# Identity products ahead of the first tile, an opening in halves, and a new order of weight blocks in a transformer trunk kernel

## The chip, the core and the metric

The kernel runs on one NeuronCore of a Trainium2 chip. The core has a matrix engine (TensorE, PE in the profile; its weight loads are shown apart as PEld), a vector engine (VectorE, DVE), a scalar engine (ScalarE, ACT), a general engine (GpSimd, POOL) and a sync engine (SyncE, SP) which issues most of the transfers. The engines run their own instruction streams in order and wait for each other through semaphores. 16 DMA engines move data between HBM, where weights and inputs lie, and the on-chip memory of 128 partitions. Matmul results go to banks of a separate accumulator memory.

The metric is the time of one execution on the device in microseconds, the median of several runs.

## What is computed

Two layers of a transformer trunk over two groups of requests, 256 and 512 rows of 1024 values, with the same weights. The first layer mixes tokens by windowed grouped attention with a sink, the second by differential attention; each is followed by a SwiGLU of hidden width 2816.

```python
def window_gqa_sink(h, w_in, w_o, sinks):
    q, k, v = jnp.split(h @ w_in, [A_Q_DIM, A_Q_DIM + A_KV_DIM], axis=-1)
    ...
    q = apply_rope(q, cos, sin) * (HEAD_DIM ** -0.5)
    k = apply_rope(k, cos, sin)
    ...
    m = jnp.maximum(jnp.max(sc, axis=-1, keepdims=True), sink)
    e = jnp.exp(sc - m)
    p = e / (jnp.sum(e, axis=-1, keepdims=True) + jnp.exp(sink - m))
    ...
    return o @ w_o

def swiglu(h, w_gate_up, w_down):
    g, u = jnp.split(h @ w_gate_up, 2, axis=-1)
    return (jax.nn.silu(g) * u) @ w_down

def trunk(x, ...):
    for i in range(DEPTH):
        h = rms_norm(x, norm_mix_pre[i])
        m = window_gqa_sink(...) if i % N_MIXERS == 0 else diff_attention(...)
        x = x + rms_norm(m, norm_mix_post[i])
        h = rms_norm(x, norm_ffn_pre[i])
        x = x + rms_norm(swiglu(h, ffn_w_gate_up[i], ffn_w_down[i]), norm_ffn_post[i])
    return x
```

## The kernel before

**Tiles and products.** The 768 rows are six tiles of 128 rows (0 and 1 the prompt, 2 to 5 the sample), in two halves of three tiles. Every fp32 product is made of three: an operand is split into a rounded part and a remainder (hi and lo), and hi·hi, lo·hi and hi·lo are summed in one bank (L376 to L378 in `product_steps`). The split of a weight block is an ACT cast (`whi`, L273) and a DVE subtraction (`wlo`, L274), together `two_parts`.

**Weight blocks.** `prepare` goes through a list of units in the order of their use. `fetch` issues the loads of the raw blocks on SP (L247) as far as buffers are free: two buffers "w" (tile name `wraw`) and two "y" (`y_wraw`), which are the scratch buffers that hold `y_pre`, `y_e` and the like at other times. A split block lies in one of RING = 5 pairs `whi`, `wlo`. `take` hands blocks to the products; `free` calls `prepare` again when a block is no longer needed, so the place of that call in the program is the place in ACT's and DVE's streams at which the next block's split stands. Units 0 to 3 are the k-v weights of the first mixer (768 columns), 4 to 12 its q and k weights, from 13 its output weights. For units 4 to 13, `whi` is not cast by ACT but loaded a second time from HBM by a converting DMA that POOL issues (L321); DVE's subtraction (L322) follows.

**Opening.** `enter(t)` normalizes a tile: sum of squares (ACT, L427), root (L420), power on POOL (L421), scaling by the row's factor and the gain `gpre` (`scaled`, DVE, L431) into `y_pre`. `transposes` turns it on PE with an identity (L469, bank `tp_h`), and the result is split again into the transposed operand (L364, L365). In the mixer tile t + 1's `entered` stands between the products of k-v unit t (`straight`), and loads the tile three ahead.

**First mixer.** `mixer_a` runs through 24 fills, groups of matmuls for k-v, q and k columns. Between these it places 96 items: each scores one head of one tile (bank `sc`, then DVE L800 and an exponential on ACT in buffer `y_e`), every second one normalizes the pair of heads two earlier (L811, L812; head one scaled on DVE, L814, head two on ACT, L815), the item four earlier is transposed (PE L832, bank `tpe`; copied to `eT` by ACT, L838), and values are summed (L847, bank `poa`). The table `marks` in `a_items` sets where items stand, in fills: item 6 stands at 9.6 of the 24 fills, item 24 at 13.7, with the others between by interpolation. `drop` frees a weight block as soon as its last product has been issued.

**Feed-forward part.** `ffn` multiplies by a scheme with seven products of quarter blocks for gate and up weights, for 11 pairs of column blocks. For the first AHEAD = 6 blocks (`for c in range(AHEAD)`) the two gate products p1 and p2 have been made earlier, and p6, p5, p7, p3, p4 follow, into the banks `py` and `pw`. They need the up block and sums of quarters of the gate and up block: `b11` (L309), `b12` (L310), `b22` (L311), `b21` (L312), made in place by DVE, with `two_parts` on them. ACT copies the results (`st` L1191, `u` L1196). The loads of gate and up blocks come in turn, all up blocks into "y" buffers but that of block c = 1.

**Tail.** The second feed-forward part ends with the last tile: `last_tile` normalizes the result by `rstd_last` and adds it to x (L568). That x is loaded by `begin(5)`, which is called inside the last product.

A scheduler keeps the order of the program on each engine but may hoist instructions whose operands allow it; `tc.issue_after(i)` puts what is issued in it behind instruction i.

Of the kernel before, what the change touches and what calls it, by code (L numbers as in the profile page):

```python
# [9 lines left out]
F32 = mybir.dt.float32  # L10
# [7 lines left out]
P = 128  # L18
# [32 lines left out]
def a_items():  # L51
# [4 lines left out]
    marks = ((0, 6.6), (6, 9.6), (24, 13.7), (48, 18.6), (72, 23.1), (76, 24))  # L56
# [32 lines left out]
def trunk(  # L89
# [107 lines left out]
    def ffn_units(layer):  # L197
        for c in range(AHEAD):
            plain(wgu[layer, c, 0], 1024)
        for c in range(NCH):  # L200
# [6 lines left out]
            raw_src.append((wgu[layer, c, 1], 1024, "w" if c == 1 else "y"))  # L207
# [30 lines left out]
    state = {"dma": 0, "split": 0, "used": 0, "w": 0, "y": 0, "tt": 0, "rb": 0, "cap": None, "behind": None, "after": None, "hold": False}  # L238
# [37 lines left out]
    def prepare(upto):  # L276

        while state["split"] < min(upto, len(units), state["cap"] or len(units)):
# [23 lines left out]
            else:  # L302
# [4 lines left out]
                b22s[i] = both[:, :512], both[:, 512:]  # L307
                two_parts(*b22s[i], b22)
                nc.vector.tensor_tensor(out=b11, in0=b12, in1=b11, op=ALU.subtract)  # L309
# [4 lines left out]
            with ExitStack() as after:  # L314
# [5 lines left out]
                if 4 <= i < N_PLAIN_A:  # L320
                    nc.gpsimd.dma_start(out=hi[:, :n], in_=raw_src[r][0])  # L321
                    state["raw_lo"] = nc.vector.tensor_tensor(  # L322
                        out=lo[:, :n], in0=src[:, :n], in1=hi[:, :n].bitcast(F32), op=ALU.subtract)
                else:
                    two_parts(hi[:, :n], lo[:, :n], src[:, :n])
# [365 lines left out]
    def mixer_a(gains, first_steps, o):  # L691
        with ExitStack() as st:
# [20 lines left out]

            def drop():
                live[0] -= 1
                free(live[0])
# [89 lines left out]
            def normalize(g, t, j):  # L806
# [7 lines left out]
                nc.vector.tensor_scalar(out=e[0], in0=e[0], scalar1=den[:, 0:1], scalar2=None, op0=ALU.mult)  # L814
# [46 lines left out]
            def item(n):  # L861
                if n < n_items:
                    score(*items[n])
                if n % 2 == 0 and 2 <= n <= n_items:
                    normalize(*items[n - 2])
                if LAG <= n < n_items + LAG:
                    turn_e(*items[n - LAG])
# [274 lines left out]
    def ffn(layer, later, comb, cpool, cstack, ostack, gains):  # L1142
# [219 lines left out]
        with ExitStack() as st:  # L1362
# [144 lines left out]
            if not final:  # L1507
# [11 lines left out]
                return {0: [do(4, 2), do(5, 1)], 1: [do(3, 3)], 2: [do(4, 3), do(5, 2)], 3: [do(5, 3)]}  # L1519
            ss4 = small.tile([P, 4], F32, tag="ss4", name="ss4")  # L1520
            junk = new_y("last")
            ss = sq[5][0]
            for k in range(2):
                last_product(2, gs, wk, last=True, parts=(k,))
                if k == 0:
                    stage(4, 1)
                    begin(5)
# [63 lines left out]
    nc.scalar.activation(out=warm, in_=mhalf[:, 0:1], func=AF.Square)  # L1591
    head = ctx.enter_context(ExitStack())
# [11 lines left out]
    def enter(t):  # L1604
        x = xs_sb[t]
        y_in[t] = new_y(f"pre0_{t}")
        scaled(y_in[t], x, row_rstd(x, y_in[t], f"pre0_{t}"), g_in)
# [10 lines left out]
    enter(0)  # L1618
    with tc.issue_after(state["rstd"].ins), tc.issue_after(state["scaled"].ins):
        prepare(2)  # L1620
    for s in transposes(y_in.pop(0), 0, "h0_0"):
        s()
# [103 lines left out]
```

## Time and profile before

| | us |
|---|---|
| runs | 1634.6, 1634.96, 1637.33 (median 1634.96) |
| profiled execution | 1637.23 |
| its span | 1635.4 |
| DVE busy in it | 1203.1 |
| ACT busy in it | 941.7 |
| POOL busy in it | 166.0 |

The span runs from the first to the last instruction that the profiler recorded; the time of the execution is 1.8 us longer. A row of the timeline gives the start and the duration in us, the engine (a q behind it marks a transfer's issue), the line, the operation, result and operands, and in brackets how long the engine was idle before it and for whom it waited. A row of the waits gives the waiting engine's line, what it waited for, the total, the number of waits and the longest. A row of the windows gives the stretch and its length, busy time and instruction count of PE, PEld, DVE, ACT and POOL, the granted PE clock, the share of the DMA engines and the traffic. The matmuls of the trace overlap, so durations of neighbours do not add up.

By the windows the first mixer's dense part, 80 to 240 us, has ACT busy for 135.70 of 160 us.

### The profile page before, as it was taken

Reading aid. Unit: us, or ns where it says so; the run is one execution under the profiler, and the core shown is the slowest. Engines: PE = TensorE matmul, PEld = TensorE weight load, DVE = VectorE, ACT = ScalarE, POOL = GpSimd, SP = SyncE. Lnnn points to the kernel's source line nnn. Section 1 sums busy time; section 2 is a strip of 40 time slices with the busy share of each in tenths; the row PEclk is TensorE's granted clock in tenths of the full one; section 3 lists DMA queues with packets and bytes.
Section 4 is the critical chain, followed back from the end, with each engine's and each line's share of the span. In section 5 each row is a group of like instructions: output and inputs, shape, how many; then the busy total and the mean of one; then the engine's idle time right before and its main releaser. Section 6 shows DMA issues by size and latency. Waiting matters only on the chain. (4 is left out here: it accounts for less than half of the span.)

```text
span 1635.4 us, 24441 instructions
## 1 busy us (share of the span) xinstructions
PE 1606.9 (98%) x9055; PEld 1491.6 (91%) x9055; DVE 1203.1 (74%) x2076; ACT 941.7 (58%) x1999; POOL 166.0 (10%) x261
## 2 busy tenths in 40 slices
PE   7999999999999999999999999999999999999998
PEld 7888778999999998888999999888999999998887
DVE  6778857878667766888585886857877667656985
ACT  5588976644444444556475666766644444444553
POOL 1121101000000000001220250421000000000000
PEclk9999999999999999999999999999999999999999
DMA  6532204443433257675432332504444432347674
GB/s 214 174 99 69 91 19 168 156 169 113 145 111 118 101 169 261 223 257 183 141 109 71 95 85 80 153 1 175 161 138 144 138 115 96 126 147 259 221 246 159
DMA packets 73383, 233.07 MB, mean 143 GB/s; under 512 B 9072, under 2 KB 17456, under 8 KB 73008
## 3 DMA queue, kind: packets, MB, share of 16 engines
q1 hardware_dynamic: 55008, 178.82, 32.1%
q0 software_dynamic: 18112, 52.44, 10.6%
q8 instruction: 71, 1.16, 0.3%
q14 instruction: 48, 0.39, 0.1%
q10 hardware_dynamic: 144, 0.26, 0.0%
HBM read 171.71 MB, written 42.86 MB: 131 GB/s over the span
## 5 line engine op out<-in xcount | busy, mean ns | idle before, releaser
L274 DVE TENSOR_TENSOR wlo<-wraw,whi 128x1024 fp32r<-128x1024 f32 (+1 forms) x159 | 188.4, 1189 | 176.7 <-ACT whi L273 175.9
L273 ACT CAST whi<-wraw 128x1024 fp32r<-128x1024 f32 (+1 forms) x159 | 162.4, 1025 | 117.5 <-PE py L377 53.1
L376 PE MATMUL py<-hhi,whi 128*128 128x384 f32 x480 | 160.8, 335 | 4.3 <-ACT u L1196 4.3
L378 PE MATMUL py<-hhi,wlo 128*128 128x384 f32 x480 | 160.3, 334 | 0.0
L377 PE MATMUL py<-hlo,whi 128*128 128x384 f32 x480 | 160.3, 334 | 0.0
L364 ACT CAST hhi<-araw 128x768 fp32r<-128x768 f32 (+1 forms) x74 | 57.5, 783 | 88.2 <-DMA araw<-act 80.8
L376 PEld LDWEIGHTS py<-hhi,whi 128*128 128x128 f32 x480 | 90.1, 188 | 5.6 <-ACT u L1196 5.6
L376 PE MATMUL pv<-whi,hhi 128*128 128x512 f32 (+1 forms) x240 | 92.4, 385 | 0.3 <-DVE yf L1408 0.3
L378 PE MATMUL pv<-whi,hlo 128*128 128x512 f32 (+1 forms) x240 | 92.2, 384 | 0.4 <-DVE hlo L365 0.4
L377 PE MATMUL pv<-wlo,hhi 128*128 128x512 f32 (+1 forms) x240 | 92.2, 384 | 0.0
L365 DVE TENSOR_TENSOR hlo<-araw,hhi 128x768 fp32r<-128x768 f32 (+1 forms) x74 | 65.2, 889 | 33.9 <-ACT hhi L364 33.6
L377 PEld LDWEIGHTS py<-hlo,whi 128*128 128x128 f32 x480 | 90.1, 188 | 0.0
L378 PEld LDWEIGHTS py<-hhi,wlo 128*128 128x128 f32 x480 | 90.1, 188 | 0.0
L1228 POOL DMA_DIRECT2D act<-st x22 | 19.3, 878 | 629.7 <-DVE st L1227 599.5
L376 PE MATMUL po<-whi,hhi 128*128 128x512 f32 x192 | 78.7, 410 | 0.0
L1023 ACT ACTIVATE be<-bsc,bmx 128x512 f32<-128x512 f32 (+1 forms) x96 | 58.8, 616 | 30.8 <-DVE bmx L1021 30.2
L376 PE MATMUL px<-hhi,whi 128*128 128x384 f32 x224 | 75.5, 337 | 0.2
L377 PE MATMUL po<-wlo,hhi 128*128 128x512 f32 x192 | 75.4, 392 | 0.0
L378 PE MATMUL po<-whi,hlo 128*128 128x512 f32 x192 | 75.2, 392 | 0.0
L378 PE MATMUL px<-hhi,wlo 128*128 128x384 f32 x224 | 74.9, 335 | 0.0
L377 PE MATMUL px<-hlo,whi 128*128 128x384 f32 x224 | 74.9, 334 | 0.0
L1021 DVE TENSOR_REDUCE bmx<-bsc 128x1 f32<-128x512 f32 (+1 forms) x96 | 55.3, 595 | 11.0 <-PE bsc L1017 10.7
(318 smaller groups left out, 4923.1 us busy)
## 6 DMA issues: line engine op xcount, KB each, us to landing
wraw<-in_wgu SPq DMA_DIRECT2D x58, 512.0 KB, 4.4
act<-st POOLq DMA_DIRECT2D x22, 1344.0 KB, 6.6
araw<-act SPq DMA_DIRECT2D x70, 384.0 KB, 3.9
y_wraw<-in_wgu SPq DMA_DIRECT2D x42, 512.0 KB, 3.8
wraw<-in_wd SPq DMA_DIRECT2D x40, 512.0 KB, 3.9
xd<-x SPq DMA_DIRECT2D x18, 512.0 KB, 2.8
x<-xd SPq DMA_DIRECT2D x18, 512.0 KB, 4.3
wraw<-in_wo SPq DMA_DIRECT2D x16, 512.0 KB, 3.5
```

What stands on the lines that cost most here:

```text
L273: state["raw_hi"] = nc.scalar.copy(out=hi, in_=src)
L274: state["raw_lo"] = nc.vector.tensor_tensor(out=lo, in0=src, in1=hi.bitcast(F32), op=ALU.subtract)
L364: state["hi"] = nc.scalar.copy(out=hi, in_=src)
L365: state["lo"] = nc.vector.tensor_tensor(out=lo, in0=src, in1=hi.bitcast(F32), op=ALU.subtract)
L376: nc.tensor.matmul(out, ah, bh, start=start and i == 0, stop=False, skip_group_check=more)
L377: nc.tensor.matmul(out, ah, bl, start=False, stop=False, skip_group_check=more)
L378: state["mm"] = nc.tensor.matmul(out, al, bh, start=False, stop=stop and i == last, skip_group_check=more)
L1021: nc.vector.tensor_reduce(out=mx, in_=s, axis=AX.X, op=ALU.max, negate=True)
L1023: nc.scalar.activation(out=e[:, :n * P], in_=s, func=AF.Exp, bias=mx, accum_out=den[:, c:c + 1])
L1228: nc.gpsimd.dma_start(out=at_hand[c // 4][:, :, c // 2 % 2], in_=out.pop(c // 2))
```

## The change

1. Twelve fp32 products of the identity with itself go to PE ahead of the first tile, into a bank of their own that nothing reads.
2. The opening works in halves: tile 0 is scaled in two halves of 512 columns, block 0 of the k-v weights is split in two halves of 384 columns, and the first half of the tile's transposes stands between these (`state["between"]`). Blocks 1 and 2 are prepared apart.
3. In the first mixer, units 5 to 8 are split as all others are, with the ACT cast in place of the converting DMA on POOL. Unit 4 and units 9 to 13 keep the DMA.
4. In the first mixer, once items run, `drop` only notes that a block is free (`owed`); the replacement is made after the next `normalize`. The DVE subtraction of the converted blocks is issued behind the scaling of `y_e` (`state["scale"]`).
5. In `marks`, item 6 moves from 9.6 to 9.9 fills.
6. In both feed-forward parts all up blocks go to "y" buffers, and from the first block on L309, the sum `b11`, stands ahead of the block's `two_parts`, issued behind the previous block's `wlo` (`state["raw_lo"]`).
7. The last tile's x is loaded before the last products into a raw weight buffer, in place of `begin(5)`.

```diff
-    marks = ((0, 6.6), (6, 9.6), (24, 13.7), (48, 18.6), (72, 23.1), (76, 24))
+    marks = ((0, 6.6), (6, 9.9), (24, 13.7), (48, 18.6), (72, 23.1), (76, 24))
...
-            raw_src.append((wgu[layer, c, 1], 1024, "w" if c == 1 else "y"))
+            raw_src.append((wgu[layer, c, 1], 1024, "y"))
...
+                with tc.issue_after(state["raw_lo"].ins) if state["after"] is not None else ExitStack():
+                    nc.vector.tensor_tensor(out=b11, in0=b12, in1=b11, op=ALU.subtract)
                 two_parts(*b22s[i], b22)
-                nc.vector.tensor_tensor(out=b11, in0=b12, in1=b11, op=ALU.subtract)
...
-                if 4 <= i < N_PLAIN_A:
+                if i == 4 or 9 <= i < N_PLAIN_A:
                     nc.gpsimd.dma_start(out=hi[:, :n], in_=raw_src[r][0])
+                    if state["scale"] is not None:
+                        after.enter_context(tc.issue_after(state["scale"].ins))
                     state["raw_lo"] = nc.vector.tensor_tensor(
                         out=lo[:, :n], in0=src[:, :n], in1=hi[:, :n].bitcast(F32), op=ALU.subtract)
                 else:
-                    two_parts(hi[:, :n], lo[:, :n], src[:, :n])
+                    for j in range(0, n, HALF if i == 0 else n):
+                        c = slice(j, j + HALF if i == 0 else n)
+                        two_parts(hi[:, c], lo[:, c], src[:, c])
+                        if i == 0 and j == 0:
+                            state["between"]()
...
+            owed = []
+
             def drop():
                 live[0] -= 1
-                free(live[0])
+                if state["scale"] is None:
+                    free(live[0])
+                else:
+                    owed.append(True)
...
-                nc.vector.tensor_scalar(out=e[0], in0=e[0], scalar1=den[:, 0:1], scalar2=None, op0=ALU.mult)
+                state["scale"] = nc.vector.tensor_scalar(out=e[0], in0=e[0], scalar1=den[:, 0:1], scalar2=None, op0=ALU.mult)
...
                     normalize(*items[n - 2])
+                    if owed:
+                        owed.clear()
+                        free(live[0])
...
+            x_of[5] = wpool.tile([P, 1024], F32, tag="wraw", name=f"x{sub}_5", bufs=RAW["w"])
+            load(x_of[5], x_at[sub][5])
...
                     stage(4, 1)
-                    begin(5)
...
+    busy = bank("busy")
+    for i in range(12):
+        nc.tensor.matmul(busy[:, :P], ident, ident, start=i == 0, stop=i == 11)
...
-        scaled(y_in[t], x, row_rstd(x, y_in[t], f"pre0_{t}"), g_in)
+        r = row_rstd(x, y_in[t], f"pre0_{t}")
+        for cols in [slice(0, 512), slice(512, D)] if t == 0 else [slice(0, D)]:
+            scaled(y_in[t][:, cols], x[:, cols], r, g_in[:, cols])
...
     enter(0)
+    state["between"], second = transposes(y_in.pop(0), 0, "h0_0")
     with tc.issue_after(state["rstd"].ins), tc.issue_after(state["scaled"].ins):
+        prepare(1)
+    with tc.issue_after(state["hi"].ins), tc.issue_after(state["lo"].ins):
         prepare(2)
-    for s in transposes(y_in.pop(0), 0, "h0_0"):
-        s()
+    second()
```

The change also moves instructions that its lines don't name. Three places follow; in the rows stand the line, the operation, the result and the operands, and a name's last number only tells tiles of one name apart. The changed file's lines have other numbers.

SP's stream in the opening, before: `x_3` is the load of tile 3, the `wraw` loads are the first two q blocks (units 4 and 5), `ropea` is a table of rotary factors.

```order
L247 DMA wraw_172<-in_waf 128x1024
L458 DMA x_3_159<-in_xs 128x1024
L247 DMA wraw_178<-in_waf 128x1024
L698 DMA ropea_238<-in_rope_b 128x768
L458 DMA x_4_267<-in_xs 128x1024
L458 DMA x_5_326<-in_xs 128x1024
```

The same place in the changed kernel:

```order
L247 DMA wraw_195<-in_waf 128x1024
L247 DMA wraw_201<-in_waf 128x1024
L705 DMA ropea_254<-in_rope_b 128x768
L465 DMA x_3_172<-in_xs 128x1024
L465 DMA x_4_283<-in_xs 128x1024
L465 DMA x_5_342<-in_xs 128x1024
```

Tile 3's load has moved from the second to the fourth place, behind the second weight block and the table.

DVE's stream in the first mixer, before, around the first scaling that ends a long wait of PE (`y_e_0_2`, L814); `wlo_863` is the subtraction of a weight block.

```order
L676 TENSOR_TENSOR qa_1_822<-zqa_1_791,qa_1_822 64x384 x2
L322 TENSOR_TENSOR wlo_863<-wraw_651,whi_862 128x1024
L663 TENSOR_TENSOR zqa_1_872<-xqa_1_868,ropea_238 128x384
L811 TENSOR_TENSOR den_0_2_832<-den_0_2_832 128x2
L800 ISA y_e_2_2_919,negm_2_2_920<-sc_2_2_916,mask,nsink 128x256
L800 ISA negm_2_2_920 128x1
L812 RECIPROCAL den_0_2_832<-den_0_2_832 128x2
L809 TENSOR_TENSOR den_1_2_880<-negm_1_2_879,sink 128x2
L666 TENSOR_TENSOR xqa_1_868<-xqa_1_868,ropea_433 128x384
L814 TENSOR_SCALAR y_e_0_2_830<-y_e_0_2_830,den_0_2_832 128x256
```

In the changed kernel the scaling is L826 and the subtraction L325:

```order
L683 TENSOR_TENSOR qa_1_832<-zqa_1_801,qa_1_832 64x384 x2
L812 ISA y_e_1_2_897,negm_1_2_898<-sc_1_2_894,mask,nsink 128x256
L812 ISA negm_1_2_898 128x1
L670 TENSOR_TENSOR zqa_1_871<-xqa_1_867,ropea_254 128x384
L823 TENSOR_TENSOR den_0_2_851<-den_0_2_851 128x2
L812 ISA y_e_1_2_897,negm_1_2_898<-sc_1_3_921,mask,nsink 128x256
L812 ISA negm_1_2_898 128x1
L824 RECIPROCAL den_0_2_851<-den_0_2_851 128x2
L673 TENSOR_TENSOR xqa_1_867<-xqa_1_867,ropea_449 128x384
L826 TENSOR_SCALAR y_e_0_2_849<-y_e_0_2_849,den_0_2_851 128x256
L325 TENSOR_TENSOR wlo_909<-wraw_667,whi_908 128x1024
```

The subtraction now stands right behind the scaling, and the items around it are one score earlier.

DVE's stream in the first feed-forward part, blocks c = 1 and 2, before. L309 to L312 are the sums, L274 the subtractions of the split, the lines above L1190 the work on the products.

```order
L309 TENSOR_TENSOR wraw_3561<-wraw_3622,wraw_3561 128x512
L274 TENSOR_TENSOR b_3681<-wraw_3622,b_3681 128x512
L310 TENSOR_TENSOR wraw_3622<-wraw_3622 128x512
L311 TENSOR_TENSOR wraw_3622<-wraw_3622,wraw_3561 128x512
L312 TENSOR_TENSOR wraw_3561<-wraw_3561,wraw_3622 128x512
L274 TENSOR_TENSOR wlo_3680<-wraw_3622,whi_3679 128x1024
L274 TENSOR_TENSOR wlo_3706<-wraw_3561,whi_3705 128x1024
L1198 TENSOR_TENSOR st_0_3703<-st_0_3703,u_0_3732 128x384
L1218 TENSOR_TENSOR u_0_3677<-pw_0_3690,u_0_3677 128x384
L274 TENSOR_TENSOR b_3780<-y_wraw_3711,b_3780 128x512
L1219 TENSOR_TENSOR st_0_3703<-u_0_3677,ga_0_3453 128x384
L309 TENSOR_TENSOR wraw_3709<-y_wraw_3711,wraw_3709 128x512
```

The same in the changed kernel:

```order
L309 TENSOR_TENSOR wraw_3577<-y_wraw_3579,wraw_3577 128x512
L372 TENSOR_TENSOR s4lo_3075<-oa_247,s4hi_3074 128x4x128
L274 TENSOR_TENSOR b_3701<-y_wraw_3579,b_3701 128x512
L311 TENSOR_TENSOR y_wraw_3579<-y_wraw_3579 128x512
L312 TENSOR_TENSOR y_wraw_3579<-y_wraw_3579,wraw_3577 128x512
L313 TENSOR_TENSOR wraw_3577<-wraw_3577,y_wraw_3579 128x512
L274 TENSOR_TENSOR wlo_3700<-y_wraw_3579,whi_3699 128x1024
L274 TENSOR_TENSOR wlo_3726<-wraw_3577,whi_3725 128x1024
L1213 TENSOR_TENSOR st_0_3723<-st_0_3723,u_0_3748 128x384
L309 TENSOR_TENSOR wraw_3640<-y_wraw_3642,wraw_3640 128x512
L1233 TENSOR_TENSOR u_0_3697<-pw_0_3710,u_0_3697 128x384
L274 TENSOR_TENSOR b_3796<-y_wraw_3642,b_3796 128x512
```

The up block of the sum for c = 1 is now in a `y_wraw` buffer, and the sum stands one row earlier, ahead of the last subtraction of the operand `s4lo`; the next block's L309 has moved up to right behind the first use of the products.

More of the change, by code (lines that the diff above doesn't have):

```diff
@@ L237, in trunk @@
     raws, parts, b22s = {}, {}, {}
-    state = {"dma": 0, "split": 0, "used": 0, "w": 0, "y": 0, "tt": 0, "rb": 0, "cap": None, "behind": None, "after": None, "hold": False}
+    state = {"dma": 0, "split": 0, "used": 0, "w": 0, "y": 0, "tt": 0, "rb": 0, "cap": None, "scale": None, "between": None, "behind": None, "after": None, "hold": False}
     tpool, dpool = [None], [None]
```

## The prediction

> **What bounds the kernel now.** I read the busy times first, then the waits of TensorE (PE), then the timeline around each wait.
>
> ```profile
> span 1635.4 us, 24441 instructions
> PE 1606.9 (98%) x9055; PEld 1491.6 (91%) x9055; DVE 1203.1 (74%) x2076; ACT 941.7 (58%) x1999; POOL 166.0 (10%) x261
> ```
>
> PE is busy for 1606.9 of 1635.4 us, so 28.5 us is all that the order of other work can win unless PE's own work changes. PE's waits say where that time lies (total, times, longest):
>
> ```profile
> PE tp_h L469 <- DVE y_pre L431: 8.0, 1, 8.0
> PE py L376 <- ACT u L1196: 4.3, 4, 1.6
> PE tpe L832 <- DVE y_e L814: 2.2, 2, 2.0
> PE tpe L832 <- ACT y_e L815: 1.2, 3, 0.6
> PE poa L847 <- ACT eT L838: 0.9, 2, 0.5
> PE sc L791 <- DVE qa L676: 0.6, 1, 0.6
> PE pw L376 <- ACT st L1191: 0.5, 1, 0.5
> ```
>
> The first is the start of the program, the tpe, poa and sc rows are the first mixer, the py and pw rows the first six blocks of the two feed-forward parts. Every part of the change aims at one of these rows, or at the tail.
>
> A wait costs PE more than its row says. Matmuls overlap:
>
> ```profile
> 12.78 0.52 PE L376 MATMUL pkva<-whi,hhi 128*128 128x384 f32 x1
> 13.10 0.52 PE L377 MATMUL pkva<-wlo,hhi 128*128 128x384 f32 x1
> ...
> 17.67 0.33 PE L376 MATMUL pkva<-whi,hhi 128*128 128x384 f32 x1
> 17.84 0.33 PE L377 MATMUL pkva<-wlo,hhi 128*128 128x384 f32 x1
> ```
>
> At full clock one starts every 0.17 us though each lasts 0.33, so a wait costs its listed idle plus 0.16. At 13 us the pitch is 0.32: PE runs at half rate there, although the clock column already reads 1.00.
>
> **Opening.** The first transposes wait for the whole normalized tile 0; the twelve identity products only fill PE's empty time ahead of them.
>
> ```profile
> 7.96 0.69 PE L469 MATMUL tp_h<-ident,y_pre 128*128 128x128 f32 x2 [7.96 <-DVE y_pre L431]
> ...
> 25.13 0.38 PE L469 MATMUL tp_h<-ident,y_pre 128*128 128x128 f32 x2
> ```
> ```profile
> 14.01 0.33 SPq L458 DMA_DIRECT2D x<-in_xs  x1
> ...
> 19.99 1.06 ACT L427 ACTIVATE y_pre<-x 128x1024 f32<-128x1024 f32 x1
> ...
> 22.47 1.28 DVE L431 SCALAR_TENSOR_TENSOR y_pre<-x,rstd_pre,gpre 128x1024 f32<-128x1024 f32 x1 [0.99 <-POOL rstd_pre L421]
> ```
> ```profile
> 18.00:21.00 3.00, 2.88 (x21) 2.57 (x20) 3.00 (x9) 2.07 (x5) 0.00 (x0) 1.00 1.03 390
> 21.00:22.00 1.00, 1.00 (x7) 1.00 (x6) 0.47 (x2) 1.00 (x6) 0.11 (x1) 1.00 0.75 290
> 22.00:23.00 1.00, 1.00 (x7) 1.00 (x7) 0.53 (x1) 0.20 (x1) 0.43 (x1) 1.00 0.19 78
> ```
>
> (In the window rows the last two columns are the DMA share and GB/s.) The halves of the first scaling bring PE's first work forward by about half of a 1.28 us pass, 0.6 us, and a shorter half-rate stretch may bring the first products forward further. But all of it ends at tile 3, whose transposes run at 25.13. Its load, issued at 14.01 ahead of a 512 KB weight block and a 384 KB rope table, now stands behind both on SP's queue. The DMA engines are full until 21 us, so 0.9 MB at 390 GB/s puts it 2.3 us later; traffic ends soon after 22. Before, the tile's square started at 19.99 and the scaling ended at 23.75, 3.76 later, of which 0.99 was a wait for POOL. The square waited for no load before, so the tile was there somewhat earlier than 19.99; I take 21.8 for it now. With 3.76 behind it, less a little of POOL's 0.99, the transposes follow at about 25.4: PE is ahead until then, waits, and goes on 0.3 later. I take **a loss of 0.3**. From the other side: if the load is not late, the 0.99 wait and the 0.58 cast that stood inside the chain are the most that can go, a gain of 1.5. At worst the tile lands at 22.3, 0.9 lost, and the wait drops the clock (1.6, next part): a loss of 2.5.
>
> [...]
>
> **First mixer to 80 us.** Three waits end here; the last drops the clock.
>
> ```profile
> 49.28 0.41 PE L376 MATMUL pqa<-hhi,whi 128*128 128x384 f32 x1 [0.15 <-DMA whi<-in_waf]
> ...
> 63.50 0.50 PE L791 MATMUL sc<-ka,qa 128*128 128x256 f32 x2 [0.62 <-DVE qa L676]
> ...
> 73.82 0.87 PE L832 MATMUL tpe<-ident,y_e 128*128 128x128 f32 x3 [1.99 <-DVE y_e L814]
> ```
> ```profile
> 70.64 1.23 DVE L322 TENSOR_TENSOR wlo<-wraw,whi 128x1024 fp32r<-128x1024 f32 x1
> ...
> 73.33 0.35 DVE L814 TENSOR_SCALAR y_e<-y_e,den 128x256 f32<-128x256 f32 x1
> ```
> ```profile
> 74.00:77.00 3.00, 3.00 (x12) 3.00 (x12) 2.08 (x9) 2.95 (x8) 1.08 (x2) 0.50 0.35 133
> 44.00:80.00 36.00, 33.24 (x201) 31.46 (x201) 27.45 (x87) 22.16 (x69) 7.54 (x14) 0.95 0.60 197
> 80.00:240.00 160.00, 157.43 (x995) 131.96 (x994) 121.23 (x422) 135.70 (x396) 18.31 (x33) 1.00 0.22 68
> ```
>
> With the pitch the waits cost 0.3, 0.8 and 2.15. After the last the granted clock is 0.50 for 3 us, which holds 1.5 us of work, about 1.6 with its edges: 4.8 in all. At 73.82 PE waits for the scaling of y_e, and 1.23 us of block subtraction stands ahead of that scaling on DVE. The change puts the subtraction behind it, and spreads the items before it over 3.3 fills instead of 3.0, which moves this transpose later. The scaling then ends about 1.2 us earlier and the 1.99 falls to about 0.7, which I take as too short for the clock to fall; the other two waits leave 0.4 of 1.1, since whi of four blocks comes from an ACT cast of a buffer already here. Four casts of 1.02 us (the group row below) make ACT's 22.16 us here 26.3 of 36, and that is the cover. Gain 4.8 − 0.7 − 0.4 = **3.7**. If the denser queue takes all but 0.5 back it is 0.5; at best 4.8.
>
> [...]
>
> ```profile
> L273 ACT CAST whi<-wraw 128x1024 fp32r<-128x1024 f32 (+1 forms) x159 | 162.4, 1025 | 117.5 <-PE py L377 53.1
> ```
>
> **80 to 240 us.** Six waits remain (the 1.2 and 0.9 rows above and 0.2 of the y_e row); with 0.16 each, 3.2 us. Subtractions behind the scalings, in the order of the new code, help the DVE one and whatever queues on DVE. But ACT scales every second head, is busy 135.70 of 160, and gets nothing off its hands. Here the new order shows no row that prices it: I take **0.8**, a quarter, with 3.2 at best; at worst the deferred blocks come late at five of the fills by 0.46 each, minus 2.3.
>
> **Feed-forward.** The second up block used to be loaded into a buffer of the gate blocks, one place later:
>
> ```profile
> 309.42 0.33 SPq L247 DMA_DIRECT2D y_wraw<-in_wgu  x1
> 310.75 0.33 SPq L247 DMA_DIRECT2D wraw<-in_wgu  x1
> ```
> ```profile
> 315.26 0.69 DVE L309 TENSOR_TENSOR wraw<-wraw,wraw 128x512 f32<-128x512 f32 x1 [1.67 <-DMA wraw<-in_wgu]
> ...
> 1174.91 0.69 DVE L309 TENSOR_TENSOR wraw<-wraw,wraw 128x512 f32<-128x512 f32 x1 [2.31 <-DMA wraw<-in_wgu]
> ...
> 1210.71 0.69 DVE L309 TENSOR_TENSOR wraw<-y_wraw,wraw 128x512 f32<-128x512 f32 x1 [5.33 <-DMA wraw<-in_wgu]
> ```
> ```profile
> 320.46 0.45 PE L376 MATMUL py<-hhi,whi 128*128 128x384 f32 x1 [1.02 <-ACT u L1196]
> ...
> 1180.10 0.44 PE L376 MATMUL py<-hhi,whi 128*128 128x384 f32 x1 [1.64 <-ACT u L1196]
> ...
> 1214.39 0.44 PE L376 MATMUL py<-hhi,whi 128*128 128x384 f32 x1 [1.46 <-ACT u L1196]
> ```
>
> Now that block takes the earlier slot, 1.33 us sooner, and DVE's 1.67 wait shrinks to 0.3. The chain behind it (sums, subtraction of wlo) fed PE's wait at 320.46. The first part's py waits are 4.3 − 1.64 − 1.46 = 1.2, with two pitches 1.5; I leave 0.3 for the new order of ACT's copies: **1.2** (0 if ACT ends last anyway, 1.5 at best).
>
> In the second part two mechanisms work. At 1174.91 it is the same load. At 1210.71 the first sum of the next block (L309) had been hoisted ahead of the last sum and the wlo of this block, waited 5.33 us for a load not needed yet, and held them. The change issues each L309 behind the previous wlo, so that such a wait stands behind what PE needs next. The waits are 1.64, 1.46 and the pw row's 0.5: with pitches 4.1. I take **3.9**, leaving 0.2. If only the pw wait goes, 0.5; at best 4.1.
>
> **Tail.** The last tile's x used to be loaded late:
>
> ```profile
> 1629.81 0.55 POOL L421 TENSOR_TENSOR rstd_last<-rstd_last,mhalf 128x1 f32<-128x1 f32 x1 [3.39 <-ACT rstd_last L420]
> ...
> 1630.94 1.41 DVE L568 SCALAR_TENSOR_TENSOR x<-yf,rstd_last,x 128x512 f32<-128x512 f32 x2 [1.14 <-DMA x<-xd]
> ```
>
> With x there, the last pass follows POOL's end at 1630.36: 0.55 at most, nothing at least; I take **0.5**.
>
> **Sum.** −0.3 + 3.7 + 0.8 + 1.2 + 3.9 + 0.5 = 9.8. The profiled execution took 1637.23 us, which gives 1627.4. It is 2.27 above the median of the runs shown, 1634.96; from that the sum gives 1625.2, or 1626.8 if those runs lacked the 1.6 of the clock's fall. I forecast **1626.0**.
>
> **Rivals.**
> - *The opening gains.* The half-rate stretch shortens and tile 3 is not late, because transfers in flight share the DMA engines. 1.2 of the 1.5 bound instead of −0.3 gives 1624.5. For it: 5.1 us or more at half pitch hold 2.6 us of work. Against it: tile 3 is now last in a full queue. [...]
> - *The mixer's waits come back elsewhere.* The denser items use up what the scaling won, the clock falls at another place, and the 3.7 + 0.8 are nothing: 1630.5. For it: DVE is busy 27.45 of 36 us, ACT 26.3 with the casts.
> - *It doesn't do what it says.* The earlier buffer frees no sooner than the old one, and the feed-forward's 5.1 stay: 1631.1. Against it: the issue at 309.42 went into just such a buffer.
> - *Slower.* The deferred block replacement and the casts put work in front of ACT's and DVE's softmax steps at each of the 48 pairs of items. PE has no slack at 98%. At 0.3 us a pair, 14.4 us turn the gain into 1640.4; the median of before is passed from 0.19 a pair, 1638.2 from 0.25. Against it: in 80 to 240 us DVE idles 38.8 us and ACT 24.3, and PE waited six times.
>
> **Chances.** Forecast 0.62, opening 0.14, mixer 0.13, not as said 0.06, slower 0.05. The range must take in the second and third rival and a bound at a time: 80 to 240 at its worst costs 3.1 more (1629.1), the second part 3.4 more (1629.4), the first mixer 3.2 more (1629.2), and the two bases are 1.6 apart. To the other side the best of 80 to 240 gives 1623.6, with the opening's best 1621.8. So **1621.0 to 1631.5**. A measurement of this kernel tells about 0.2% from no change, 3.3 us: faster is below 1631.7, which the forecast, both gaining rivals and the mixer's meet, and most of the fourth: 0.88. Within 0.2%: 0.07. Slower, above 1638.2: 0.05.
>
> **What would show it.** Right: tile 3's transposes near 25.4 with a PE wait ahead of them; no granted clock of 0.50 near 75; no py wait over 0.4; an L568 row released by POOL. Wrong: new tpe or sc waits of a microsecond between 44 and 240, an L309 wait that still ends a PE wait, or transposes of tile 3 at 26 or later with the half pitch behind them.

## The result, and the profile after

| | runs | median, us | range, us |
|---|---|---|---|
| before | 6 | 1635.39 | 1634.6 to 1637.33 |
| changed | 6 | 1629.2 | 1625.55 to 1629.48 |

The ratio of the times is 0.9949, 95% interval 0.9938 to 0.9960: faster by 0.5%, 6.2 us between the medians. The profiled executions are 8.1 us apart (1637.23 and 1629.1). The forecast was 1626.0 with a range of 1621.0 to 1631.5; the median lies in it, 3.2 above the forecast.

The head of the page of the changed kernel (busy time, share and instructions of each engine):

```profile
span 1627.1 us, 24494 instructions
PE 1606.3 (99%) x9079; PEld 1492.8 (92%) x9079; DVE 1204.4 (74%) x2078; ACT 944.2 (58%) x2004; POOL 168.3 (10%) x257
```

PE is busy for the same time as before, though it has the identity products to do as well (24 rows of the trace, 5.5 us, in time that was empty). What fell is idle time. PE's waits in the changed kernel, over the whole span (total, times, longest):

```profile
PE tp_h L476 <- DVE y_pre L438: 3.8, 4, 2.0
PE busy L1610 <- POOL ident masks.py:199: 1.7, 1, 1.7
PE tpe L844 <- DVE y_e L826: 1.5, 2, 1.3
PE tp_h L476 <- DVE y_pd L438: 1.4, 1, 1.4
PE tpe L844 <- DVE den L821: 0.9, 1, 0.9
PE pv L383 <- DVE yf L1423: 0.8, 2, 0.5
PE pw L383 <- ACT st L1206: 0.7, 2, 0.4
```

The py row (4.3 us in four waits) is gone, and sc is too. tp_h now has four waits in the opening, one of 2.0 us at tile 3. The tpe row on den is new: a wait of 0.87 us at 78.48, in the first mixer. The two rows on y_pd and yf, which belong to places that the change doesn't touch, have grown.

To read where the time went, I take the **lead**: the start of a PE instruction in the profile of before minus the start of the same instruction in another profile. It is positive where the other kernel is ahead. The places are tile 3's transposes (before: 25.13), the first product of the second q block (49.28), two scores (100.02 and 201.06), a product of the first feed-forward part (352.63), the first product past 800, and the wait of the second part (1214.39). At these places every kernel's stream on PE has the same instructions behind it. Between 49 and 96 us that isn't so, since the table `marks` and the deferral shift the items against the products: the score at 81.15 comes six instructions later in the changed kernel. The figures 1.1 and 2.85 in the expectations below are leads read at 81 us; the lead is read at 100 here, and no wait of PE lies between 82 and 100 us in either kernel.

| kernel | tile 3 | 49 | 100 | 201 | 353 | 800 | 1214 | time (runs) |
|---|---|---|---|---|---|---|---|---|
| changed | −1.0 | −0.5 | 1.8 | 4.0 | 5.1 | 4.3 | 8.4 | 1629.2 (6) |
| f0_changed_again | −2.2 | −3.2 | −1.4 | 0.7 | 1.6 | 1.3 | 4.9 | 1629.03 (7) |
| e1_no_identity | 1.7 | 1.7 | 2.9 | 3.4 | 4.4 | 6.5 | 9.7 | 1627.26 (4) |
| e2_tile3_first | −0.5 | 0.0 | 2.4 | 4.5 | 5.9 | 8.0 | 11.8 | 1626.21 (5) |
| f1_tile3_first_again | −0.8 | −1.8 | 0.2 | 2.6 | 3.8 | 5.9 | 10.1 | 1626.82 (5) |
| e2b_tile3_first_no_identity | 1.4 | 0.6 | 2.9 | 3.2 | 4.3 | 5.5 | 9.5 | 1628.13 (4) |
| f2_no_identity_marks96 | 1.7 | 0.9 | 2.4 | 4.6 | 5.7 | 5.6 | 9.6 | 1627.22 (5) |
| e3_dma_whi | −0.6 | −1.9 | −0.8 | 1.4 | 2.5 | 2.5 | 6.6 | 1630.08 (1) |
| e4_marks96 | −0.4 | 0.0 | 1.9 | 3.8 | 4.9 | 6.9 | 11.1 | 1626.0 (1) |
| e5_free_at_drop | −0.9 | −0.4 | 1.8 | 1.2 | 2.2 | 4.0 | 8.0 | 1628.74 (1) |
| e6_up1_w | −0.9 | −2.0 | −0.8 | 1.0 | 0.0 | 0.1 | 2.1 | 1634.62 (1) |
| e7_sum_behind | −0.9 | −0.5 | 1.7 | 3.9 | 4.1 | 4.2 | 7.4 | 1629.32 (1) |
| f3_x5_late | −0.7 | −0.3 | 1.9 | 4.0 | 5.1 | 4.8 | 8.6 | 1629.34 (1) |

Each row is one profiled execution, so stages that a kernel shares with others tell how much a stage scatters. From 353 to 800 all of them run the same instructions, and the step of the lead there lies between −0.8 (changed) and +2.1 (e1, e2). No part of the change is read off that stage.

### The profile page after: what moved, and what is told of

Same layout as the page of the kernel before. It is cut to its first block, busy times and chain, and to the rows that moved or that the text cites. A ratio compares the mean times of both kernels' runs of the same rounds, so it can differ in the third digit from the quotient of the medians.

```text
span 1627.1 us, 24494 instructions
## 1 busy us (share of the span) xinstructions
PE 1606.3 (99%) x9079; PEld 1492.8 (92%) x9079; DVE 1204.4 (74%) x2078; ACT 944.2 (58%) x2004; POOL 168.3 (10%) x257
## 5 line engine op out<-in xcount | busy, mean ns | idle before, releaser
L274 DVE TENSOR_TENSOR wlo<-wraw,whi 128x1024 fp32r<-128x1024 f32 (+2 forms) x162 | 191.1, 1183 | 186.0 <-ACT whi L273 185.0
L273 ACT CAST whi<-wraw 128x1024 fp32r<-128x1024 f32 (+2 forms) x162 | 164.8, 1020 | 109.6 <-PE py L384 53.1
L274 DVE TENSOR_TENSOR wlo<-y_wraw,whi 128x1024 fp32r<-128x1024 f32 x44 | 53.8, 1223 | 13.8 <-ACT whi L273 13.7
```

Of the source, the lines that this page charges most:

```text
L273: state["raw_hi"] = nc.scalar.copy(out=hi, in_=src)
L274: state["raw_lo"] = nc.vector.tensor_tensor(out=lo, in0=src, in1=hi.bitcast(F32), op=ALU.subtract)
```

## Experiments

Times of the kernel before beside them: median 1636.35 (9 runs) with e1 to e3, 1635.56 (1 run) with e4 to e7, 1636.95 (12 runs) with f0 to f3. A kernel of one run is read by its profile only.

### e1_no_identity: without the identity products

```diff
-    busy = bank("busy")
-    for i in range(12):
-        nc.tensor.matmul(busy[:, :P], ident, ident, start=i == 0, stop=i == 11)
```

> The changed kernel without its twelve identity products, nothing else. Theory A (the products open the clock, but the opening ends at tile 3's load): the first k-v products run at a pitch of 0.32 us again until about 13 to 16 us, yet tile 3's transposes start within 0.3 us of the changed kernel's 26.16, because that tile lands at 22.2 in both, and PE's wait ahead of them shrinks from 2.0 to under 1; the time stays within 0.5 us of the changed kernel's. Theory B (the early clock is worth its time): the transposes start 1 to 2 us later, and the time grows by as much.

Both theories failed, at their common ground that tile 3 lands at the same time. Rows of the opening's timeline without the products (the issues on SP, the square of tile 3 on ACT, its transposes on PE):

```profile
13.64 0.33 SPq L465 DMA_DIRECT2D x<-in_xs  x1
14.02 0.42 SPq L247 DMA_DIRECT2D wraw<-in_waf  x1
14.50 0.44 SPq L705 DMA_DIRECT2D ropea<-in_rope_b  x1
...
18.65 1.06 ACT L434 ACTIVATE y_pre<-x 128x1024 f32<-128x1024 f32 x1 [0.20 <-DMA x<-in_xs]
...
23.48 0.38 PE L476 MATMUL tp_h<-ident,y_pre 128*128 128x128 f32 x2
```

The same rows of the changed kernel:

```profile
10.89 1.30 SPq L247 DMA_DIRECT2D wraw<-in_waf  x2
13.22 0.33 SPq L705 DMA_DIRECT2D ropea<-in_rope_b  x1
13.64 12.73 SPq L465 DMA_DIRECT2D x<-in_xs  x3
...
22.25 1.06 ACT L434 ACTIVATE y_pre<-x 128x1024 f32<-128x1024 f32 x1 [3.28 <-DMA x<-in_xs]
...
26.16 0.52 PE L476 MATMUL tp_h<-ident,y_pre 128*128 128x128 f32 x3 [1.99 <-DVE y_pre L438]
```

In both, tile 3's load is issued at 13.64, about when its buffer comes free (in the changed kernel tile 1's scaling on DVE, which reads that buffer, runs from 12.15 to 13.43). With the identity products the two others stand ahead of it and the tile is there at 22.25, without them at 18.65. So it is the identity products, not the halves, that put the load last. Why the order of SP's queue changes with them, no run shows. The transposes start 2.7 us earlier without the products.

And the products' own worth is small. Without them the half pitch (0.32 us from product to product) lasts until 11.33, 4.0 us from the first transposes at 7.31, in place of none:

```profile
10.70 0.53 PE L384 MATMUL pkva<-wlo,hhi 128*128 128x384 f32 x1
11.02 0.53 PE L385 MATMUL pkva<-whi,hlo 128*128 128x384 f32 x1
11.33 0.44 PE L383 MATMUL pkva<-whi,hhi 128*128 128x384 f32 x1
11.61 0.34 PE L384 MATMUL pkva<-wlo,hhi 128*128 128x384 f32 x1
11.79 0.34 PE L385 MATMUL pkva<-whi,hlo 128*128 128x384 f32 x1
```

Yet the lead near 16 us is 1.6 here and 1.8 in the changed kernel, because the full pitch there (0.17 us) runs into waits for the splits of the first operands (0.26, 0.16 and 0.45 us). The time, 1627.26, is 0.9944 of the kernel before (0.9930 to 0.9957); the changed kernel has 0.9949 in its own runs, so the medians don't tell them apart.

### e2_tile3_first: the load's place alone

```diff
-            load(raw[:, :n], src)
+            with tc.issue_after(state["x"].ins) if i == 5 else ExitStack():
+                load(raw[:, :n], src)
...
-        nc.sync.dma_start(out=x, in_=x_at[sub][t])
+        state["x"] = nc.sync.dma_start(out=x, in_=x_at[sub][t])
...
-                nc.sync.dma_start(out=full[:, :2 * HALF], in_=rope_b[len(tab)])
+                with tc.issue_after(state["x"].ins) if not tab else ExitStack():
+                    nc.sync.dma_start(out=full[:, :2 * HALF], in_=rope_b[len(tab)])
```

> The changed kernel with tile 3's load ahead of the second q block and of the table on SP's queue, as before. Theory A (the load's place costs the opening): the tile lands at about 19, PE has no wait at its transposes, which start at about 24.0 in place of 26.16; the time falls by 1.5 to 2.2 us against the changed kernel. Rival: the chain of square, root, power and scaling is as late as the load, or the second q block is late instead; the transposes start at 25 or later, or a new wait of PE stands between 28 and 45, and the time falls by less than 0.7.

The tile was there by 19.6, but the transposes started at 25.67 and not at 24.0. The wait moved one product up. DVE and PE of this kernel:

```profile
22.18 1.28 DVE L439 SCALAR_TENSOR_TENSOR y_pre<-x,rstd_pre,gpre 128x1024 f32<-128x1024 f32 x1 [0.66 <-POOL rstd_pre L429]
...
23.58 0.68 DVE L373 TENSOR_TENSOR hlo<-tp_h,hhi 128x512 fp32r<-128x512 f32 x1
```
```profile
24.32 0.44 PE L386 MATMUL pkva<-whi,hlo 128*128 128x384 f32 x1 [1.79 <-DVE hlo L373]
```

Tile 3's scaling now stands ahead of a remainder of tile 2 on DVE, and PE waits for that remainder. By its profile the rival is right: the start is at 25 or later. The time of 1626.21 fell all the same, by more than the rival's 0.7, for reasons that lie behind the opening (a lead of 8.0 at 800 us against 4.3), so it is no proof of theory A.

### e2b_tile3_first_no_identity: both

> Both of these edits. If the early clock only shows where tile 3 is in time (theory A), tile 3's transposes start 1.0 to 1.8 us later than with the identity products kept, at 25 to 25.8, and the time is about 1 to 1.8 us above that kernel's. If the products do nothing for the opening in any case, both kernels have the same start of these transposes to 0.3.

Neither theory foresaw it: the transposes start at 23.73, 1.9 us earlier than in e2. Without the identity products the scheduler leaves the remainder ahead of the scaling. The median is 1.9 above e2's, near what theory A said, but the intervals overlap (0.9936 to 0.9963 and 0.9926 to 0.9953), and its reason doesn't hold, since the opening was faster.

### e3_dma_whi: the converting DMA for units 5 to 8

```diff
-                if i == 4 or 9 <= i < N_PLAIN_A:
+                if 4 <= i < N_PLAIN_A:
```

> The changed kernel with whi of units 5 to 8 loaded by the converting DMA again. Theory A (these loads fed part of the waits before 80 us): the wait at the first product of a q block near 49 us returns with 0.1 to 0.5 us, and the lead over the kernel before at the scores near 81 us falls by 0.3 to 1 us. Rival (the place of the DVE subtraction did it all): the lead there is unchanged to 0.2, and ACT is busy about 4 us less between 44 and 80.

ACT is busy 20.17 us between 44 and 80 in place of 25.59, so the casts are what they were taken for. The lead can't be compared with the changed kernel's as it stands, since this execution had already lost 1.3 us between tile 3 and 31 us, where the clock fell (0.81 from 24 to 28 us and 0.77 from 28 to 32). The kernel that stands level with it is f1 (e2's once more, below), which lost as much there and has the casts: −1.8 at 49 us against −1.9. From there to 100 us f1 gains 2.0 and e3 1.1. The wait near 49 that theory A named doesn't return; the loss lies at the scaling of y_e. The subtraction of a block waits for the converting DMA in e3 and not in f1, and PE's wait behind it is longer. DVE and PE of e3, then of f1:

```profile
68.59 1.23 DVE L325 TENSOR_TENSOR wlo<-wraw,whi 128x1024 fp32r<-128x1024 f32 x1 [0.51 <-DMA whi<-in_waf]
```
```profile
75.24 0.66 PE L844 MATMUL tpe<-ident,y_e 128*128 128x128 f32 x4 [2.44 <-DVE y_e L826]
```
```profile
67.57 1.22 DVE L326 TENSOR_TENSOR wlo<-wraw,whi 128x1024 fp32r<-128x1024 f32 x1
```
```profile
74.22 0.66 PE L846 MATMUL tpe<-ident,y_e 128*128 128x128 f32 x4 [1.57 <-DVE y_e L828]
```

So the casts are likely worth about 0.9 us, theory A's size by another mechanism. It rests on one execution of each. e6 has the casts and gains 1.2 only, but there the clock fell behind this wait (0.71 from 74 to 77 us).

### e4_marks96: the table alone

```diff
-    marks = ((0, 6.6), (6, 9.9), (24, 13.7), (48, 18.6), (72, 23.1), (76, 24))
+    marks = ((0, 6.6), (6, 9.6), (24, 13.7), (48, 18.6), (72, 23.1), (76, 24))
```

> The changed kernel with item 6 back at 9.6 fills. Theory A (the table's move is part of the gain before 80 us, since it puts the first transposes of y_e later): PE's wait for y_e near 72 us grows from 1.3 to 1.8 or more and the lead over the kernel before at the scores near 81 us falls from 1.1 by 0.5 to 2 us, with the half clock back behind it if the wait passes 2. Rival (the subtraction's new place is enough): the wait stays within 0.3 of 1.3 and the lead within 0.4.

The rival, as far as it goes. The wait for y_e is 1.6, and a wait for qa (0.8) is back, while the den wait of the changed kernel is gone. The lead goes up by 1.9 between 49 and 100, against 2.3 in the changed kernel and 1.8 in its second profile f0, and stands at 3.8 against 4.0 at 201. The table moves waits from one place to another; its worth isn't seen.

### e5_free_at_drop: the deferral alone

```diff
-                if state["scale"] is None:
-                    free(live[0])
-                else:
-                    owed.append(True)
+                free(live[0])
```

> The changed kernel with a block's replacement issued at the drop again, in place of behind the next normalize. Theory A (the deferral is what takes the splits off the way of the scalings): the waits of tpe and poa between 80 and 240 us go from the changed kernel's 0.5 back to 1.5 to 2.5, and the lead gained between 81 and 201 us falls from 2.85 to under 1.5. Rival (the items' spacing and the ACT casts did that): the lead gained there stays at 2.4 or more.

Theory A. PE's waits between 80 and 240 us in this kernel:

```profile
PE tpe L841 <- ACT y_e L824: 1.1, 3, 0.5
PE tpe L841 <- DVE y_e L823: 0.9, 2, 0.7
PE poa L856 <- ACT eT L847: 0.7, 2, 0.4
```

and in the changed kernel:

```profile
PE poa L859 <- ACT eT L850: 0.3, 1, 0.3
PE tpe L844 <- DVE y_e L826: 0.2, 1, 0.2
```

Six waits of 2.7 us against two of 0.5. From 100 to 201 us the lead falls by 0.6 here, where it rises by 2.2 in the changed kernel (2.15 before rounding): the deferral is worth 2.7 there, read from one execution, and without it the rest of the change loses a little. Up to 100 it is worth nothing, 1.8 in both: one y_e wait of 2.15 stands here for the changed kernel's two of 1.25 and 0.87. Its 2.7 are more than half of what the mixer brought.

### e6_up1_w: the up block's buffer

```diff
-            raw_src.append((wgu[layer, c, 1], 1024, "y"))
+            raw_src.append((wgu[layer, c, 1], 1024, "w" if c == 1 else "y"))
```

> The changed kernel with the up block of c = 1 back in a gate buffer. Theory A (its earlier slot is the whole gain of the first feed-forward part): the wait of py for u near 320 us is back with 0.8 to 1.1, the lead gained between 317 and 353 falls from 1.5 to 0.3 or less, and in the second part the wait near 1180 is back with 1.2 to 1.7, while the waits near 1189 and 1214 stay away. Rival (the order of the sums does it): both parts keep their gains to 0.3.

The waits are back, with more than before (PE rows of both parts):

```profile
320.74 0.44 PE L383 MATMUL py<-hhi,whi 128*128 128x384 f32 x1 [1.72 <-ACT u L1211]
...
1180.45 0.44 PE L383 MATMUL py<-hhi,whi 128*128 128x384 f32 x1 [1.71 <-ACT u L1211]
```

From 201 us to 353 the lead falls from 1.0 to 0.0, where the changed kernel's rises from 4.0 to 5.1: undoing the slot costs 2.1 there. In the second part the lead rises by 1.8 (0.3 at 1150 to 2.1) in place of 3.9, again 2.1 less. The waits near 1189 and 1214 stay away: theory A. In the first part the new order of the sums without the earlier slot is even 1.0 us slower than the kernel before.

### e7_sum_behind: the sums' order

```diff
-                with tc.issue_after(state["raw_lo"].ins) if state["after"] is not None else ExitStack():
-                    nc.vector.tensor_tensor(out=b11, in0=b12, in1=b11, op=ALU.subtract)
                 two_parts(*b22s[i], b22)
+                nc.vector.tensor_tensor(out=b11, in0=b12, in1=b11, op=ALU.subtract)
```

> The changed kernel with the sum b11 behind two_parts, free to be hoisted, as before. Theory A (the hoisted sum blocks DVE only where its load is late): the waits near 1189 and 1214 in the second part come back with 0.4 to 1.5 each, 2 to 2.5 in all of the 3.9 there; the first part keeps its gain to 0.3. Rival (the up block's slot also ends those): the second part keeps 3.5 or more.

Mostly the rival. The second part keeps 3.0 of 3.9 (the kernels that keep both edits gain 3.4 to 4.0 there), and what it loses, 0.9, lies near 1175 (a py wait of 0.64) and not at 1189 or 1214. The first part loses 0.9 as well (from 201 to 353 the lead rises by 0.2 in place of 1.1; 0.9 to 1.4 in the kernels with both), against theory A. DVE still waits with the sum hoisted:

```profile
1202.65 0.69 DVE L309 TENSOR_TENSOR wraw<-y_wraw,wraw 128x512 f32<-128x512 f32 x1 [3.60 <-DMA wraw<-in_wgu]
```

but PE no longer waits for what stands behind it. This kernel's lead just ahead of that place is 5.8, so by PE's progress the row's 1202.65 stands for 1208.4 in the kernel before, whose same row started at 1210.71: the wait ends 2.3 us earlier, more than the 1.46 that PE had waited. So each of the two edits alone ends the wait at 1214, one by an earlier load, one by the order.

### f0_changed_again, f1_tile3_first_again, f2_no_identity_marks96

f0 is the changed kernel, f1 is e2's, f2 has the edits of e1 and of e4.

> The changed kernel as it is, on the chip of the next three, as their standard. Its wait of about 2 us ahead of tile 3's transposes was followed by a granted clock under 0.85 in two of six profiles that had this wait. If that draw makes its spread, its runs lie in two groups some 1 to 3 us apart; median 1628 to 1630 where the kernel before has 1635 to 1636.

> Tile 3's load ahead of the second q block and of the table, with the identity products, once more beside the changed kernel. Its wait moved to a product that needs hlo of tile 2 (1.8 us), so theory A (the load's place is worth little since the wait only moves, and the mixer takes back what the opening wins): the same as the changed kernel to 1 us. Rival (worth its 2 us): 1.5 to 2.5 us faster.

> The changed kernel without the identity products and with item 6 back at 9.6 fills. No wait of PE in the opening, tile 3's transposes near 23.5. If the mixer takes the lead back (theory A), the lead over the kernel before is 1.5 to 2.7 at tile 3 and 3 to 4 at the scores near 201 us, as with the identity products, and the time is at most 2 us under the changed kernel's. Rival (a lead in the opening stays): the lead near 201 us is 5.5 or more.

| | us | ratio to the kernel before, 95% interval |
|---|---|---|
| f0 | 1629.03 (1626.94 to 1634.75) | 0.9959, 0.9944 to 0.9973 |
| f1 | 1626.82 (1625.35 to 1629.84) | 0.9945, 0.9933 to 0.9957 |
| f2 | 1627.22 (1625.62 to 1628.84) | 0.9943, 0.9930 to 0.9956 |

f1 and f2 lie some 2 us under the changed kernel, for f1 what the rival said; the intervals overlap, so that is likely and not settled. f2 started tile 3's transposes at 23.46, 1.7 ahead of the kernel before, and its lead near 201 is 4.6, between the bounds of its two theories, against 4.0 in the changed kernel that began 2.7 behind it. e1, as early, stands at 3.4. So the stages behind take most of an opening's lead back. In f2 1.1 us of it go at once, where the first q block's product waits for wlo (28.88), and the mixer's waits for y_e end when DVE is ready, however early PE is (e1, 2.2 ahead of the changed kernel at 49 us, waits 2.34 there in place of 1.25). f0's median came as expected; its runs spread over 8 us, not in two groups.

The clock can be a part of that spread: the slowest run has the lowest mean granted clock (0.995) and the fastest the highest (1.000), though a run at 0.997 took only 1627.53. The window from 28 to 32 us of the changed kernel (length, then busy time and count of PE, PEld, DVE, ACT and POOL, the granted clock, DMA share and GB/s) in its first profile:

```profile
28.00:32.00 4.00, 4.00 (x26) 3.97 (x25) 3.61 (x10) 2.48 (x8) 0.66 (x1) 1.00 0.47 154
```

and in that of f0, the same program:

```profile
28.00:32.00 4.00, 4.00 (x19) 4.00 (x17) 4.00 (x9) 2.20 (x5) 0.00 (x0) 0.57 0.39 139
```

Both have a wait of about 2 us ahead of tile 3's transposes (f0 is 1.1 us later at that place already, with its tile there at 23.37 in place of 22.25). Of ten profiles with such a wait in the opening (1.8 to 2.1 us), four show a clock under 0.85 right behind it (at the lowest of the windows from 24 to 28 and 28 to 32 us: e3 0.77, e6 0.64, f0 0.57, f1 0.75), and lose 1.3 to 1.4 us of lead between tile 3 and 31 us, where the other six gain 0.2. The three profiles without that wait (e1, e2b, f2) show 1.00. Why the clock falls behind this wait in some executions and not in others, no run shows.

### f3_x5_late: the tail

```diff
-            x_of[5] = wpool.tile([P, 1024], F32, tag="wraw", name=f"x{sub}_5", bufs=RAW["w"])
-            load(x_of[5], x_at[sub][5])
...
+                    begin(5)
```

> The changed kernel with the last tile's x loaded inside the last product, as before. Theory A (that load ended last): the last addition waits for it again, and the time from the last product's addition to the end of the last addition grows by 0.5 to 0.6. Rival (POOL's power ends last anyway): it grows by less than 0.2.

The last addition in the changed kernel, and without the early load:

```profile
1622.66 1.42 DVE L575 SCALAR_TENSOR_TENSOR x<-yf,rstd_last,x 128x512 f32<-128x512 f32 x2 [0.59 <-POOL rstd_last L428]
```
```profile
1622.89 1.42 DVE L575 SCALAR_TENSOR_TENSOR x<-yf,rstd_last,x 128x512 f32<-128x512 f32 x2 [1.33 <-DMA x<-xd]
```

From the last product's addition (1620.58 and 1620.06) to the end of these rows it takes 3.50 and 4.25 us: theory A, with 0.75.

## Why the prediction came out as it did

Its terms against the steps of the lead in the changed kernel's profile:

| term | foreseen | measured | from |
|---|---|---|---|
| opening, to 49 us | −0.3 | −0.5 | −1.0 at tile 3, half of it made up |
| first mixer, to 80 | 3.7 | 2.3 | −0.5 to 1.8, read at 100 |
| 80 to 240 | 0.8 | 2.3 | 1.8 to 4.1 |
| first feed-forward part | 1.2 | 1.0 | 4.1 to 5.1 at 353 |
| 353 to 1150 | none | −0.6 | 5.1 to 4.5 |
| second feed-forward part | 3.9 | 3.9 | 4.5 to 8.4 |
| 1214 to the last product | none | −0.6 | 8.4 to 7.7 |
| tail | 0.5 | 0.5 | 7.7 to 8.3 |
| sum | 9.8 | 8.3 | |

**Opening.** The mechanism was right (a load behind two others in a full queue, ahead of a wait at tile 3), and it was a little too small: the transposes started at 26.16, not 25.4, since the tile landed at 22.2, near the upper end of what was allowed for. A part of that is transfer time left unused, which the prediction's full queue had no place for: between 13 and 15 us the DMA engines move 76 and 125 GB/s at shares of 0.29 and 0.40, before 195 and 337 GB/s. What leaves it unused is open. The cause of the load's place was missed: "the twelve identity products only fill PE's empty time", but they also move the load, and without them the opening is 1.7 ahead at tile 3 (e1). The clock's fall, kept as the bad end, came in one profile of the program (0.57 from 28 to 32 us in f0) and not in the other (1.00).

**First mixer and 80 to 240.** Together 4.5 were foreseen and 4.6 came, but not where they were foreseen, so the agreement of the sum is in part luck. To 80 us the step that was mis-sized is "The scaling then ends about 1.2 us earlier and the 1.99 falls to about 0.7". The subtraction did go behind the scaling, and the scaling ends 1.13 us earlier (72.55 against 73.68). Yet the wait is still 1.25, and a second one follows that no term had:

```profile
72.20 0.35 DVE L826 TENSOR_SCALAR y_e<-y_e,den 128x256 f32<-128x256 f32 x1
72.46 1.22 DVE L325 TENSOR_TENSOR wlo<-wraw,whi 128x1024 fp32r<-128x1024 f32 x1
```
```profile
72.61 0.66 PE L844 MATMUL tpe<-ident,y_e 128*128 128x128 f32 x4 [1.25 <-DVE y_e L826]
...
78.48 0.63 PE L844 MATMUL tpe<-ident,y_e 128*128 128x128 f32 x4 [0.87 <-DVE den L821]
```

PE came to the first of these 0.47 us earlier than before, since the wait for qa ahead of it had gone: gains at two waits in a row for the same engine were added, though the second wait grows by what the first one gives. DVE hardly stops there, as this window shows (the third pair of numbers is DVE's busy time and count):

```profile
68.00:72.00 4.00, 3.35 (x23) 3.15 (x21) 3.77 (x14) 3.92 (x12) 0.00 (x0) 1.00 0.69 212
```

With the pitch, PE's waits from 44 to 80 us fell from 3.2 to 2.4 us, by 0.8 and not 2.1; the rest of the 2.3 is the half clock that did not come (1.6 by the prediction's sum). That it did not come is in part luck: the clock stayed at 1.00 behind 2.15 us in e5, 2.34 in e1 and 2.44 in e3, and it stood at 0.71 from 74 to 77 us behind 1.83 in e6. That 0.7 us is too short for a fall was the prediction's estimate; behind the wait of 0.87 at 78.48 the clock read 1.00. No run undoes the subtraction's place alone, so its 1.13 us is read from these rows, and the casts have a share in it (e3). In 80 to 240 the prediction took a quarter of 3.2 because no row priced the deferral; e5 prices it at 2.7.

**Feed-forward parts.** Sizes as forecast, the mechanisms half right. The first part was given to the load alone, but the load without the order gains 0.2 there (e7) and the order without the load loses 1.0 (e6): it takes both. "In the second part two mechanisms work" holds, and undoing the load's slot costs 2.1 us there, undoing the order of the sums 0.9; but at 1214, which the prediction gave to the order, either would do.

**Tail.** As forecast; undoing it costs 0.75.

**What was not foreseen** are two losses where nothing was changed: tp_h behind y_pd near 734, and a wait of pv near 1597. Both scatter between executions of the same instructions; the first is absent in seven of the thirteen profiles, the second in all but two. What draws them was not tried. The rest of the distance to the forecast is its base: the profile of before was 1.8 above the median of the six runs, while that of the changed kernel was at its median, so medians show 6.2 of the 8.1.

**The rivals.** The opening did not gain. The mixer's waits came back in part, at the same place and at 78.48, and used up 1.4 of the 3.7. The feed-forward part did what it says. The price of a pair for the slower rival was negative: the deferral took waits away. Of the signs, those for "right" came: a PE wait ahead of tile 3's transposes, no granted clock of 0.50 near 75, no py wait over 0.4, and an L568 row (now L575) released by POOL. Two of those for "wrong" came in part: the new tpe wait of 0.87, and transposes of tile 3 past 26, behind which a granted clock of 0.57 stood in f0.

## What to carry to other kernels

Where one engine is full and another waits for it several times in a row, the gains at these waits can't be added: what the first gives, the next takes, until the full engine itself is done earlier. Here the urgent step ended earlier by nearly the whole length of the row that was moved behind it, and the wait shrank by 0.74 us of 1.99. Moving every replacement behind the urgent step, as the deferral does, gave over three times the 0.8 us that its stretch was thought to offer. Edits can also need each other: in the first feed-forward part the load's slot alone won 0.2 us and the order of the sums alone lost 1.0, where both won 1.0. Work put into an idle engine can be free there and still cost elsewhere, when the order of another queue changes with it (here 5.5 us of products in PE's empty time, and a tile that is there 3.6 us later): compare the order of all queues, the transfers' first. And a lead won at the start is worth only what the next full engine lets through (f2, 2.7 us ahead of the changed kernel at tile 3, is 0.6 ahead at 201 us); measure it behind that engine.

## What was not expected of the hardware

A wait of PE of about 2 us in the opening was followed by a granted clock of 0.57 to 0.77 in four profiles of ten (f0, e6, f1, e3), at 1.3 to 1.4 us a time, and by 1.00 in the other six. Near 72 us the clock fell behind waits of 1.99 (before, 0.50 from 74 to 77 us) and 1.83 us (e6, 0.71 there), and stayed at 1.00 behind 2.15, 2.34 and 2.44 (e5, e1, e3). The half pitch at the start, 0.32 us from product to product in place of 0.17, lasted 8 us before (7.96 to 16), 4.0 without the identity products but with the opening in halves (7.31 to 11.33), and was over by the first k-v product with them (the one at 9.21 lasts 0.33 us, where those at half pitch last 0.52). A tile's load issued at the same 13.64 was there at 18.65 or at 22.25, by its place in a queue whose 0.9 MB ahead of it had to pass first, at some 400 GB/s from 16 to 22 us, behind a stretch from 13 to 15 us with the DMA engines partly idle (shares 0.29 and 0.40).
